# A two-layer hybrid network: modulation weights in 512 KB halves, output weights split over the last attention head, the dt turn one z block later

## The chip, the cores and the metric

The kernel runs on one core of one Trainium2 chip. The metric is the device time of one execution in microseconds. Engines are TensorE (PE; its weight loads are PEld), VectorE (DVE), ScalarE (ACT), GpSimd (POOL) and SyncE (SP, which here only issues transfers). ScalarE issues transfers too, in the order of its other instructions.

## The reference

The network has two layers on 256 context and 1024 latent tokens of width 1024. Before each layer a modulation vector is computed from a conditioning vector, for latent and for context tokens:

```
def modulation(cvec, w, b):
    m = jax.nn.silu(cvec) @ w + b
    return jnp.split(m, 3, axis=-1)          # shift, scale, gate
...
u_lat = rms_norm(h_lat, g_pre[i]) * (1.0 + sc[:, None]) + sh[:, None]
...
h_lat = h_lat + gt[:, None] * rms_norm(y_lat, g_post[i])
```

Layer 0 projects u with one weight matrix into six parts. Two (xr, gr) feed a gated linear recurrence in both directions (four tiles of 128 channels), four (q, k, v, gd) a differential attention with four heads:

```
s = jnp.einsum("bqhcd,bkhcd->bhcqk", q, k).astype(jnp.float32) * (DA_HEAD_DIM ** -0.5)
p = jax.nn.softmax(s, axis=-1)
w = p[:, :, 0] - lam * p[:, :, 1]
...
y_l = jnp.concatenate([r_l * jax.nn.silu(gr_l), head_norm(o_l) * jax.nn.silu(gd_l)], axis=-1) @ w_out
```

Layer 1 projects into z, x, B, C and dt (dt through a softplus) and runs a chunked state-space scan (32 heads, chunks of 128) in both directions, then a gated norm and an output projection. The output is the latent stream.

## The kernel before

Arithmetic is float32. A projection (`proj`, line 321) makes three products per weight tile: operand and weight are each split in a high part, which TensorE multiplies in its faster 32-bit format, and a low remainder: high x high, low x high and high x low. The names end in H and L, or begin with wh and wl. Each output block of 512 tokens is 24 such matmuls of 512 columns, the context block 24 of 256 columns. The split itself is a cast on ScalarE (line 298) and a subtraction on VectorE (line 299), after a 512 KB load on SyncE into a two-buffer staging pool (`wst`).

The order of each engine's instructions is made by a list scheduler with a cost model, from the program's text; pools with a set number of buffers, in SBUF and PSUM, make an instruction wait until the last reader of a buffer's former tile is done. On the chip every engine and every issuing queue works in the order it was given.

`backbone` first computes the modulation of layer 0 (`modulation`, lines 135 to 184), then u, then the four recurrence tiles (`lru_in`, `lru_scan`). Between the first two scans the text has `gate_rows` (lines 187 to 205), which computes the gate part of both layers' modulation, and after the second scan the rest of layer 1's modulation. Both make, per step k of 8, four products of 32 stationary columns each (the conditioning vectors, padded) with 512 weight columns; product j writes partitions 32j to 32j + 31 of one PSUM tile and uses only 32 of TensorE's columns. They are plain float32, so each is two records in the trace. Each of the four weight tiles of a step is a 256 KB load on SyncE into the pool `wmod1` with five buffers. The tail of `gate_rows` handles four pieces of 512 columns: copy from PSUM, add the bias, multiply by the post-norm weight (both loaded by ScalarE's queue into the single buffer `gbm`), store to DRAM on SyncE. The piece's own tile has the tag "u" with one buffer, and so has the row `mrow` that layer 1's modulation copies out of PSUM before TensorE transposes it (line 170).

`v_block` (line 473) projects v and transposes it in three groups, each into a PSUM tile of the rotating `c.psum`; for head 0 it first issues one dummy matmul (`fill`, line 228).

`attention_head` (lines 530 to 641) goes over ten query tiles: scores, row maxima on VectorE (lines 578, 579, 583), exponentials on ScalarE (585, 586), the weighted difference on VectorE (598), transposes (608) and the product with v (612). In the last head, `between()` runs once, at query tile 5: it issues the last gate block (`gd_block`, whose matmuls serve as work between tiles), closes the pools of layer 0's inputs, and loads and splits the eight row blocks of the output weights, 512 KB each through two staging buffers: cast on VectorE (line 1427), remainder on GpSimd (line 1428).

In layer 1, `dt_block` (lines 658 to 725) computes the dt tables and returns `turn`, which transposes them (line 717); the text has one `z_block` ahead of `turn` and seven behind it.

Of the kernel before, what the change touches and what calls it, by code (L numbers as in the profile page):

```python
# [19 lines left out]
P = 128  # L20
# [113 lines left out]

def modulation(c, a, layer, wpool, tmp, ahead=None, between=None):
# [9 lines left out]
    for hf in range(parts):  # L145
        pm = c.pm()
        for k in range(KT):
# [6 lines left out]
            else:  # L154
                for j in range(4):
                    wm = wpool.tile([P, cw], F32, name=f"wm{layer}_{j}{k}", tag="wm")
                    nc.sync.dma_start(wm, src[:, j // 2, cw * (j % 2) : cw * (j % 2) + cw])
                    cols.append(wm)
            if ahead:
                ahead(hf, k)  # L160
            for j in range(4):
                w = cols[j // 2][:, cw * (j % 2) : cw * (j % 2) + cw] if parts == 2 else cols[j]
                nc.tensor.matmul(pm[32 * j : 32 * j + 32, 0:cw], c.sc[:, k, :], w, start=(k == 0), stop=(k == KT - 1))
# [7 lines left out]
        if layer == 0 and hf == 0:  # L171
            c.turned = last_pe(nc)
        pv = pc[:, 0:cw].rearrange("p (q j r) -> p j q r", q=nq, r=32)
# [13 lines left out]
def gate_rows(c, a, wpool, tmp):  # L187
    nc = c.nc
    pm = c.pm()
    for k in range(KT):  # L190
        for j in range(4):
            w = wpool.tile([P, 512], F32, name=f"wg{j}_{k}", tag="wm")
            o = 2 * D + 512 * (j % 2)
            nc.sync.dma_start(w, a["w_mod"][j // 2, k * P : (k + 1) * P, o : o + 512])
            nc.tensor.matmul(pm[32 * j : 32 * j + 32, :], c.sc[:, k, :], w, start=(k == 0), stop=(k == KT - 1))
    for j in range(4):
        layer, n = j // 2, slice(512 * (j % 2), 512 * (j % 2) + 512)
        row = tmp.tile([P, 512], F32, name=f"grow{j}", tag="u", bufs=1)[0:2, :]
        nc.vector.tensor_copy(row, pm[32 * j : 32 * j + 2, :])
        for q, src, op in ((0, a["b_mod"][layer : layer + 1, 2 * D + n.start : 2 * D + n.stop], OP.add),  # L200
                           (1, a["g_post"][layer : layer + 1, n], OP.mult)):
            bm = tmp.tile([2, 512], F32, name=f"gbm{j}{q}", tag="gbm", bufs=1)
            nc.scalar.dma_start(bm, src.to_broadcast([2, 512]))
# [269 lines left out]
def v_block(c, w, uH, uL, pool, apool, name):  # L473
# [4 lines left out]
    for j0, n in ((0, 4), (4, 4), (8, 2)):  # L478
        ps = c.psum()
        if name == "0" and j0 == 0:  # L480
            fill(c, ps, FILL[3])
# [48 lines left out]
def attention_head(c, h, kk, v, pool, spool, scores, dr, between=None):  # L530
# [105 lines left out]
    for qt in range(NT):  # L636
        nxt = front(qt + 1) if qt + 1 < NT else None
        if qt == 5 and between:
            between()
        back(qt, weigh(qt, *fr))  # L640
        fr = nxt
# [160 lines left out]
def layer1(c, a, uH, uL, U, out, dram, h_d, psm, xdt):  # L802
# [17 lines left out]
    with ExitStack() as s1:  # L820
        c.wpools = [(U.enter_context(tc.tile_pool(name=f"wst1{i}", bufs=1)), U.enter_context(tc.tile_pool(name=f"wsp1{i}", bufs=1))) for i in range(2)]
        c.wcyc = 0
        with tc.tile_pool(name="dtp", bufs=1, side="right") as dp:
            tabs, turn = dt_block(c, a, xdt, dp, scst, dr)
            z_block(c, a, 0, uH, uL, zp, dr)
# [3 lines left out]
        for i in range(1, nz):  # L829
# [743 lines left out]
```

## Time and profile before

| quantity | value |
|---|---|
| median of 3 runs | 1819.09 us (1819.03 to 1819.13) |
| profiled execution | 1822.81 us |
| its span | 1820.8 us |
| mean granted TensorE clock | 0.987 of full speed |
| TensorE / VectorE / ScalarE / GpSimd busy | 1749.1 / 1136.4 / 814.3 / 497.1 us |

The span is the stretch from the first to the last recorded instruction; the execution's own time is 2 us longer. Busy time of TensorE counts pipelined matmuls with their modelled ends, so one record may be longer than the distance to the next. A row's bracket names the idle time of the engine just before it and what released it.

### The profile page before, as it was taken

Reading aid. Unit: us, or ns where it says so; the run is one execution under the profiler, and the core shown is the slowest. Engines: PE = TensorE matmul, PEld = TensorE weight load, DVE = VectorE, ACT = ScalarE, POOL = GpSimd, SP = SyncE. Lnnn points to the kernel's source line nnn. Section 1 sums busy time; section 2 is a strip of 40 time slices with the busy share of each in tenths; the row PEclk is TensorE's granted clock in tenths of the full one; section 3 lists DMA queues with packets and bytes.
Section 4 is the critical chain, followed back from the end, with each engine's and each line's share of the span. In section 5 each row is a group of like instructions: output and inputs, shape, how many; then the busy total and the mean of one; then the engine's idle time right before and its main releaser. Section 6 shows DMA issues by size and latency. Waiting matters only on the chain. (4 is left out here: it accounts for less than half of the span.)

```text
span 1820.8 us, 24369 instructions
## 1 busy us (share of the span) xinstructions
PE 1749.1 (96%) x8968; PEld 1344.8 (74%) x8968; DVE 1136.4 (62%) x1646; ACT 814.3 (45%) x1599; POOL 497.1 (27%) x467
## 2 busy tenths in 40 slices
PE   6999999999999997999999999999999899999997
PEld 2665377788888886886788888888787577776765
DVE  3735366785838577566736767666221766778797
ACT  4542455374636464444434444445311554343443
POOL 1201000100000004110006766767401443443342
PEclk8999999999999998999999999999999999999999
DMA  7434513532222315342235757576954677776664
GB/s 246 149 100 150 174 61 123 148 93 76 90 58 70 102 44 179 116 139 81 85 112 157 233 156 231 159 217 168 317 176 139 222 247 248 258 265 244 243 228 140
DMA packets 269244, 293.44 MB, mean 161 GB/s; under 512 B 16905, under 2 KB 213518, under 8 KB 268614
## 3 DMA queue, kind: packets, MB, share of 16 engines
q1 hardware_dynamic: 240944, 262.73, 45.7%
q10 hardware_dynamic: 28182, 29.16, 4.9%
q8 instruction: 71, 1.16, 0.3%
q14 instruction: 47, 0.39, 0.1%
HBM read 187.49 MB, written 100.42 MB: 158 GB/s over the span
## 5 line engine op out<-in xcount | busy, mean ns | idle before, releaser
L350 DVE SCALAR_TENSOR_TENSOR xbc<-xp_xb,pb,xbc 128x1283 f32<-128x1283 f32 (+1 forms) x72 | 141.7, 1972 | 2.8
L769 POOL TENSOR_TENSOR x2w<-tok_x,wd 128x1152 f32<-128x1152 f32 (+2 forms) x48 | 119.2, 2508 | 48.3 <-ACT tok_x L749 48.3
L967 POOL TENSOR_TENSOR s<-s,etb 128x512 f32<-128x512 f32 x64 | 69.2, 1082 | 184.5 <-DVE s L968 91.6
L623 POOL TENSOR_TENSOR ors<-z,mhalf 128x4 f32<-128x4 f32 (+1 forms) x12 | 13.8, 1146 | 351.9 <-DVE z L621 285.3
L1146 PE MATMUL psap<-wo1l,yh 128*128 128x512 f32 x256 | 101.6, 397 | 3.2 <-DVE wo1l L1040 3.2
L778 POOL TENSOR_TENSOR x2l<-x2w,x2h 128x1152 fp32r<-128x1152 f32 x32 | 103.6, 3258 | 0.5 <-DMA d_x<-x2l 0.5
L348 DVE TENSOR_SCALAR xbc<-xp_xb,pb 128x1283 f32<-128x1283 f32 (+1 forms) x24 | 29.9, 1245 | 116.2 <-ACT xp_xb L340 94.3
L1146 PE MATMUL psap<-wo1h,yh 128*128 128x512 f32 x256 | 101.8, 400 | 0.2 <-DVE acc L1156 0.2
L1146 PE MATMUL psap<-wo1h,yl 128*128 128x512 f32 x256 | 101.5, 396 | 0.0
L321 PE MATMUL pscp<-u1H,wh_xb 128*128 128x512 f32 x232 | 92.2, 398 | 0.0
L321 PE MATMUL pscp<-u1H,wl_xb 128*128 128x512 f32 x232 | 92.0, 397 | 0.0
L321 PE MATMUL pscp<-u1L,wh_xb 128*128 128x512 f32 x232 | 91.8, 396 | 0.0
L968 DVE TENSOR_TENSOR s<-s,psat 128x512 f32<-128x512 f32 x64 | 43.6, 681 | 74.0 <-PE psat L956 71.2
L321 PE MATMUL psap<-u1H,wl_z 128*128 128x512 f32 x224 | 89.3, 399 | 0.0
L321 PE MATMUL psap<-u1L,wh_z 128*128 128x512 f32 x224 | 89.2, 398 | 0.0
L321 PE MATMUL psap<-u1H,wh_z 128*128 128x512 f32 x224 | 89.2, 398 | 0.0
L585 ACT ACTIVATE p<-scores,nm 128x1024 f32<-128x1024 f32 x64 | 71.5, 1117 | 29.5 <-DVE nm L584 20.3
L560 PE MATMUL scores<-kk,xq 128*128 128x512 f32 (+1 forms) x208 | 77.4, 384 | 1.7 <-ACT p L585 1.5
L777 ACT CAST x2h<-x2w 128x1152 fp32r<-128x1152 f32 x32 | 37.2, 1161 | 89.2 <-POOL x2w L769 89.2
L956 PE MATMUL psat<-x,bk 128*128 128x512 f32 x216 | 72.1, 437 | 2.5 <-DMA x<-d_x 1.2
L561 PE MATMUL scores<-kk,xl 128*128 128x512 f32 (+1 forms) x208 | 72.9, 364 | 0.0
L612 PE MATMUL psat<-v,wT 128*128 128x128 f32 x572 | 71.4, 278 | 0.0
(487 smaller groups left out, 5115.0 us busy)
## 6 DMA issues: line engine op xcount, KB each, us to landing
x<-d_x SPq DMA_DIRECT2D x72, 512.0 KB
d_x<-x2h SPq DMA_DIRECT2D x32, 576.0 KB
d_x<-x2l SPq DMA_DIRECT2D x32, 576.0 KB
wst_xb<-in_o_w_in_dram SPq DMA_DIRECT2D x24, 512.0 KB
d_acc<-acc SPq DMA_DIRECT2D x24, 512.0 KB
acc<-d_acc SPq DMA_DIRECT2D x24, 512.0 KB
wm<-in_w_mod_dram SPq DMA_DIRECT2D x16, 512.0 KB
wg<-in_w_mod_dram SPq DMA_DIRECT2D x32, 256.0 KB
```

The costliest lines, as they stand in the source:

```text
L321: nc.tensor.matmul(ps[:n, :w_], l[:, k, :], r[:, k, t0 : t0 + w_], start=(k == 0 and i == 0), stop=(k == KT - 1 and i == 2))
L350: nc.vector.scalar_tensor_tensor(out[:, j0 : j0 + n], xp[:, j0 + k : j0 + k + n], cw(k), out[:, j0 : j0 + n], OP.mult, OP.add)
L560: nc.tensor.matmul(out, xq[m][:, qs], kk[m][:, k0 : k0 + n], start=True, stop=False)
L561: nc.tensor.matmul(out, xl[:, m, qs], kk[m][:, k0 : k0 + n], start=False, stop=True)
L585: nc.scalar.activation(pr[m][:, NCTX:], scores[m], AF.Exp, bias=nm[:, m : m + 1], accum_out=zz[:, 1, m : m + 1])
L612: nc.tensor.matmul(po[:, :P], wT[:, j, :], v[:, j, :], start=(j == 0), stop=(j == nkt - 1))
L769: nc.gpsimd.tensor_tensor(x2[:, o : o + n, :].rearrange("p c (h e) -> p c h e", e=64), t[:, a0:a1, :].rearrange("p c (h e) -> p c h e", e=64),
L778: nc.gpsimd.tensor_tensor(l, x2, h.bitcast(F32), OP.subtract)
L956: nc.tensor.matmul(ps, bk[:, l, t, :], x2[:, r, :], start=(i == 0), stop=(i == 2))
L967: nc.gpsimd.tensor_tensor(sn, self.prev[g, d], self.et[:, hs, t : t + 1].to_broadcast([P, 8, 64]), OP.mult)
L968: nc.vector.tensor_tensor(sn, sn, psv, OP.add)
L1146: nc.tensor.matmul(po, l[:, q, :], w[:, n], start=(q == 0 and i == 0), stop=(q == 3 and i == 2))
```

## The change

It has seven parts.

1. Modulation of layer 1 and gate rows load per step two tiles of 512 KB [128 x 1024] instead of four of 256 KB; the pool `wmod1` has three buffers instead of five. A new function `together` issues product 2 first and asks the scheduler to put products 3, 0 and 1 right behind it.
2. The tail of `gate_rows` handles eight pieces of 256 columns instead of four of 512. The bias row and the post-norm row are loaded into the second half of the piece's own tile; `gbm` is gone.
3. One dummy matmul (`FILL[3]` is 1) moves from `v_block` of head 0 to the end of layer 0's modulation.
4. The third group of transposes of `v_block` of head 0 goes to a tile of `c.pm()`.
5. In the last head the gate block and the pools open at query tile 3, and the eight weight blocks are issued at tiles 3 to 8.
6. Their high part is cast by ScalarE, their remainder subtracted by VectorE.
7. Two z blocks stand ahead of the dt `turn` in the text.

```diff
+def together(c, product):
+    product(2)
+    with c.tc.issue_after(last_pe(c.nc)):
+        for j in (3, 0, 1):
+            product(j)
...
-                for j in range(4):
-                    wm = wpool.tile([P, cw], F32, name=f"wm{layer}_{j}{k}", tag="wm")
-                    nc.sync.dma_start(wm, src[:, j // 2, cw * (j % 2) : cw * (j % 2) + cw])
+                for i in range(2):
+                    wm = wpool.tile([P, D], F32, name=f"wm{layer}_{i}{k}", tag="wm")
+                    nc.sync.dma_start(wm, src[:, i, :])
                     cols.append(wm)
...
         if layer == 0 and hf == 0:
             c.turned = last_pe(nc)
+        elif layer == 0:
+            fill(c, c.pm(), FILL[3])
...
-    for j in range(4):
-        layer, n = j // 2, slice(512 * (j % 2), 512 * (j % 2) + 512)
-        row = tmp.tile([P, 512], F32, name=f"grow{j}", tag="u", bufs=1)[0:2, :]
-        nc.vector.tensor_copy(row, pm[32 * j : 32 * j + 2, :])
+    for j, o in ((j, o) for j in range(4) for o in (0, 256)):
+        layer, n = j // 2, slice(512 * (j % 2) + o, 512 * (j % 2) + o + 256)
+        t = tmp.tile([P, 512], F32, name=f"grow{j}{o}", tag="u", bufs=1)
+        row = t[0:2, 0:256]
+        nc.vector.tensor_copy(row, pm[32 * j : 32 * j + 2, o : o + 256])
         for q, src, op in ((0, a["b_mod"][layer : layer + 1, 2 * D + n.start : 2 * D + n.stop], OP.add),
                            (1, a["g_post"][layer : layer + 1, n], OP.mult)):
-            bm = tmp.tile([2, 512], F32, name=f"gbm{j}{q}", tag="gbm", bufs=1)
-            nc.scalar.dma_start(bm, src.to_broadcast([2, 512]))
+            bm = t[0:2, 256:512]
+            nc.scalar.dma_start(bm, src.to_broadcast([2, 256]))
             nc.vector.tensor_tensor(row, row, bm, op)
...
     for j0, n in ((0, 4), (4, 4), (8, 2)):
-        ps = c.psum()
-        if name == "0" and j0 == 0:
-            fill(c, ps, FILL[3])
+        ps = c.pm() if name == "0" and j0 == 8 else c.psum()
...
-        if qt == 5 and between:
-            between()
+        if between:
+            between(qt)
...
-            z_block(c, a, 0, uH, uL, zp, dr)
+            for i in range(2):
+                z_block(c, a, i, uH, uL, zp, dr)
...
-    wm = s4.enter_context(tc.tile_pool(name="wmod1", bufs=5))
+    wm = s4.enter_context(tc.tile_pool(name="wmod1", bufs=3))
...
-        for k in range(KT):
-            st = W.mp.tile([P, D], F32, name=f"wos{k}", tag="xr")
-            nc.sync.dma_start(st, wo[:, k, :])
-            nc.vector.tensor_copy(W.h[:, k, :], st)
-            nc.gpsimd.tensor_tensor(W.l[:, k, :], st, W.h[:, k, :].bitcast(F32), OP.subtract)
+
+    def split_wo(k):
+        st = W.mp.tile([P, D], F32, name=f"wos{k}", tag="xr")
+        nc.sync.dma_start(st, wo[:, k, :])
+        nc.scalar.copy(W.h[:, k, :], st)
+        nc.vector.tensor_tensor(W.l[:, k, :], st, W.h[:, k, :].bitcast(F32), OP.subtract)
+
+    def last_head(qt):
+        if qt == 3:
+            open_out()
+        for k in {3: (0,), 4: (1,), 5: (2,), 6: (3, 4), 7: (5, 6), 8: (7,)}.get(qt, ()):
+            split_wo(k)
```

Three places show how the instructions move. Line numbers of the changed kernel are some 13 to 23 higher. First TensorE in the gate rows, at step k = 3 of before: wg0_3 to wg3_3 are the step's four weight tiles, psbp is the projection of the third recurrence tile.

```order
L195 MATMUL psat57_1111<-wg0_3_1148,silu_c_125 32x512
L195 MATMUL psat57_1111<-wg1_3_1151,silu_c_125 32x512
L321 MATMUL psbp58_1255<-u0L_75,wh_xr2_1251 128x256
L321 MATMUL psbp59_1281<-u0H_74,wh_xr2_1251 128x512
L321 MATMUL psbp59_1281<-u0H_74,wl_xr2_1252 128x512
L321 MATMUL psbp59_1281<-u0L_75,wh_xr2_1251 128x512
L195 MATMUL psat57_1111<-wg2_3_1154,silu_c_125 32x512
L321 MATMUL psbp59_1281<-u0H_74,wh_xr2_1251 128x512
L321 MATMUL psbp59_1281<-u0H_74,wl_xr2_1252 128x512
L321 MATMUL psbp59_1281<-u0L_75,wh_xr2_1251 128x512
L195 MATMUL psat57_1111<-wg3_3_1157,silu_c_125 32x512
```

The same step after, where wg1_3 holds the columns of products 2 and 3 and wg0_3 those of 0 and 1:

```order
L338 MATMUL psbp60_1271<-u0H_74,wh_xr2_1241 128x512
L338 MATMUL psbp60_1271<-u0H_74,wl_xr2_1242 128x512
L338 MATMUL psbp60_1271<-u0L_75,wh_xr2_1241 128x512
L208 MATMUL psbm58_1113<-wg1_3_1140,silu_c_125 32x512 x2
L208 MATMUL psbm58_1113<-wg0_3_1138,silu_c_125 32x512 x2
L338 MATMUL psbp60_1271<-u0H_74,wh_xr2_1241 128x512
L338 MATMUL psbp60_1271<-u0H_74,wl_xr2_1242 128x512
```

The four products, in three runs before, stand in one run. Over both stages the 20 and 22 runs become 9 and 10, and between two runs of the steady part stand 12 to 15 matmuls of the projection.

Second VectorE at the tail of the gate rows. Before, with the pieces grow0 and grow1:

```order
L199 COPY grow0_1208<-psat57_1111 2x512
L442 TENSOR_TENSOR a200_1088<-a200_1088,sg_gr0_488 128x1024
L204 TENSOR_TENSOR grow0_1208<-grow0_1208,gbm00_1210 2x512
L348 TENSOR_SCALAR xc2_1333<-xp_xr2_1244,pa_116 128x1283
L299 TENSOR_TENSOR wl_xr3_1636<-wst_xr3_1633,wh_xr3_1635 128x1024
L350 SCALAR_TENSOR_TENSOR xc2_1333<-xp_xr2_1244,pa_116,xc2_1333 128x1283
L358 SCALAR_TENSOR_TENSOR sg_gr2_1248<-th_gr2_0_1369,psbp61_1344 128x256
L350 SCALAR_TENSOR_TENSOR xc2_1333<-xp_xr2_1244,pa_116,xc2_1333 128x1283
L204 TENSOR_TENSOR grow0_1208<-grow0_1208,gbm01_1213 2x512
```

After, with the pieces grow00 and grow0256, halves of the former first piece:

```order
L216 COPY grow00_1178<-psbm58_1113 2x256
L367 SCALAR_TENSOR_TENSOR xc2_1323<-xp_xr2_1234,pa_116,xc2_1323 128x1283
L221 TENSOR_TENSOR grow00_1178<-grow00_1178 2x256
L367 SCALAR_TENSOR_TENSOR xc2_1323<-xp_xr2_1234,pa_116,xc2_1323 128x1283
L375 SCALAR_TENSOR_TENSOR sg_gr2_1238<-th_gr2_0_1359,psbp62_1334 128x256
L316 TENSOR_TENSOR wl_xr3_1594<-wst_xr3_1591,wh_xr3_1593 128x1024
L221 TENSOR_TENSOR grow00_1178<-grow00_1178 2x256
L375 SCALAR_TENSOR_TENSOR sg_gr2_1238<-th_gr2_256_1387,psbp63_1362 128x512
L216 COPY grow0256_1185<-psbm58_1113 2x256
```

The operand gbm is gone, since the loaded row lies in the piece's own tile; eight such sequences run down VectorE's list, the last of them behind the rotary work of head 0's queries. On TensorE the transposes of the modulation's row, 12 projection matmuls behind the last run before, stand 127 instructions behind it.

Third VectorE in the last head. Before, around query tile 8 (nl and nm are row maxima, wos0 a staged weight block):

```order
L578 TENSOR_REDUCE nl3_8_0_6079<-scores0_2385 128x1
L1427 CAST wo0H_5885<-wos0_5893 128x1024
L594 TENSOR_TENSOR Z3_5442<-zz3_7_5976 128x2
L596 RECIPROCAL rz3_7_6091<-Z3_5442 128x1
L1427 CAST wo0H_5885<-wos1_5897 128x1024
```

After, where the first weight block is met at query tiles 5 and 6:

```order
L599 TENSOR_TENSOR nm3_5_5755<-nm3_5_5755,nl3_5_1_5772 128x1
L1445 TENSOR_TENSOR wo0L_5708<-wos0_5715,wo0H_5707 128x1024
L628 COPY oall3_5397<-psap301_5808 128x128
L593 TENSOR_REDUCE nl3_6_0_5847<-scores0_2342 128x1
L1445 TENSOR_TENSOR wo0L_5708<-wos1_5782,wo0H_5707 128x1024
```

The first two blocks move up by some two query tiles. At the dt turn the order of the transposes among TensorE's instructions is the same in both kernels: they stand behind the matmuls of four z blocks.

## Rows read from the trace of the kernel before

**Rows 1.** Page of before, part 1: engine, busy us (share of the span), instructions.

```profile
PE 1749.1 (96%) x8968; PEld 1344.8 (74%) x8968; DVE 1136.4 (62%) x1646; ACT 814.3 (45%) x1599; POOL 497.1 (27%) x467
```

**Rows 2.** Timeline of PE, gate-row products: start, us, line, operation.

```profile
152.80 0.40 PE L321 MATMUL psbp<-u0H,wl_xr 128*128 128x512 f32 x1
153.03 0.40 PE L321 MATMUL psbp<-u0L,wh_xr 128*128 128x512 f32 x1
153.36 1.05 PE L195 MATMUL psat<-wg,silu_c 128*32 128x512 f32 x4
154.34 0.50 PE L321 MATMUL psbp<-u0H,wh_xr 128*128 128x512 f32 x1
154.68 0.39 PE L321 MATMUL psbp<-u0H,wl_xr 128*128 128x512 f32 x1
```

**Rows 3.** Timeline of PE: a block of four products; two gate products.

```profile
184.16 1.06 PE L163 MATMUL psbm<-wm,silu_c 128*32 128x512 f32 x8
...
119.70 1.99 PE L415 MATMUL psbt<-xc,bdi 128*128 128x512 f32 x4
```

**Rows 4.** Lines 195 and 163: count, ns min/median/max, first and last start.

```profile
L195 PE MATMUL psat<-wg,silu_c x64: 592/592/617, 121.6 to 163.4; 128*32 128x512 f32 x64
...
L163 PE MATMUL psbm<-wm,silu_c x64: 592/605/617, 182.1 to 227.8; 128*32 128x512 f32 x64
```

**Rows 5.** Timeline, two large transfers (640 and 512 KB) and their waiters.

```profile
681.10 0.32 SPq L524 DMA_DIRECT2D d_sgd<-sg_gd  x1
684.09 0.81 SPq L1426 DMA_DIRECT2D wos<-in_e_w_out_dram  x2
...
693.30 3.33 SPq L1426 DMA_DIRECT2D wos<-in_e_w_out_dram  x2
...
700.30 2.78 DVE L1427 CAST wo0H<-wos 128x1024 fp32r<-128x1024 f32 x1 [0.20 <-DMA wos<-in_e_w_out_dram]
```

**Rows 6.** Timeline, 4 KB transfers of the gate-row pieces and their waiters.

```profile
185.10 0.40 ACTq L203 DMA_DIRECT2D gbm<-in_g_post_dram  x1
...
187.63 0.68 DVE L204 TENSOR_TENSOR grow<-grow,gbm 2x512 f32<-2x512 f32 x1 [1.14 <-DMA gbm<-in_g_post_dram]
192.62 0.69 DVE L199 COPY grow<-psat 2x512 f32<-2x512 f32 x1 [4.31 <-DMA d_grow<-grow]
...
190.44 0.26 SPq L205 DMA_DIRECT2D d_grow<-grow  x1
...
203.67 0.45 SPq L205 DMA_DIRECT2D d_grow<-grow  x1
```

**Rows 7.** Timeline of PE, stops around the second scan and the value block.

```profile
279.00 0.50 PE L321 MATMUL psbp<-u0H,wh_gd 128*128 128x512 f32 x1 [3.04 <-DVE sg_gd L358]
...
331.53 0.48 PE L483 MATMUL psbt<-ident,vt 128*128 128x128 f32 x2 [2.65 <-ACT v L484]
```

**Rows 8.** Timeline of PE, first projection of layer 0.

```profile
56.42 0.39 PE L321 MATMUL psbp<-u0H,wh_xr 128*128 128x256 f32 x1 [1.16 <-ACT u0H L259]
```

**Rows 9.** Timeline of DVE, last head: casts, a slowed operation, a subtract.

```profile
690.11 0.68 DVE L1427 CAST wo0H<-wos 128x1024 fp32r<-128x1024 f32 x1
690.98 2.84 DVE L1427 CAST wo0H<-wos 128x1024 fp32r<-128x1024 f32 x1
...
713.74 2.26 DVE L619 SCALAR_TENSOR_TENSOR z<-Z 128x4 f32<-128x4 f32 x1
...
717.76 1.21 DVE L1443 TENSOR_TENSOR mx<-mx,mh 128x1024 fp32r<-128x1024 f32 x1
```

**Rows 10.** Window of the last head: length, PE, PEld, DVE, ACT, POOL, clock, DMA.

```profile
690.00:720.00 30.00, 20.54 (x106) 17.04 (x105) 29.21 (x38) 13.13 (x32) 15.46 (x7) 0.79 0.54 173
```

**Rows 11.** Timeline of ACT, last head: its wait before the last square.

```profile
725.15 0.31 ACT L615 ACTIVATE oj<-oall 128x128 f32<-128x128 f32 x1 [3.96 <-POOL wo0L L1428]
```

**Rows 12.** Timeline of PE, first transposes of the dt tables.

```profile
903.12 0.40 PE L717 MATMUL pscu<-ident,rmask 64*128 64x64 f32 x3 [1.43 <-ACT rmask L702]
```

More of the change, by code (lines that the diff above doesn't have):

```diff
@@ L160, in modulation, with product @@
                 ahead(hf, k)
-            for j in range(4):
-                w = cols[j // 2][:, cw * (j % 2) : cw * (j % 2) + cw] if parts == 2 else cols[j]
-                nc.tensor.matmul(pm[32 * j : 32 * j + 32, 0:cw], c.sc[:, k, :], w, start=(k == 0), stop=(k == KT - 1))
+            def product(j):
+                nc.tensor.matmul(pm[32 * j : 32 * j + 32, 0:cw], c.sc[:, k, :], cols[j // 2][:, cw * (j % 2) : cw * (j % 2) + cw],
+                                 start=(k == 0), stop=(k == KT - 1))
+            together(c, product)
         mrow = tmp.tile([P, 512], F32, name=f"mrow{layer}{hf}", tag="u")[:, 0:cw]
@@ L190, in gate_rows, with product @@
     for k in range(KT):
[L191 to L196, printed above, removed]
-        layer, n = j // 2, slice(512 * (j % 2), 512 * (j % 2) + 512)
-        row = tmp.tile([P, 512], F32, name=f"grow{j}", tag="u", bufs=1)[0:2, :]
-        nc.vector.tensor_copy(row, pm[32 * j : 32 * j + 2, :])
+        wm = []
+        for layer in range(2):
+            w = wpool.tile([P, D], F32, name=f"wg{layer}_{k}", tag="wm")
+            nc.sync.dma_start(w, a["w_mod"][layer, k * P : (k + 1) * P, 2 * D : 3 * D])
+            wm.append(w)
+        def product(j):
+            nc.tensor.matmul(pm[32 * j : 32 * j + 32, :], c.sc[:, k, :], wm[j // 2][:, 512 * (j % 2) : 512 * (j % 2) + 512],
+                             start=(k == 0), stop=(k == KT - 1))
+        together(c, product)
+    for j, o in ((j, o) for j in range(4) for o in (0, 256)):
[3 more added lines that the diff above has]
+        nc.vector.tensor_copy(row, pm[32 * j : 32 * j + 2, o : o + 256])
         for q, src, op in ((0, a["b_mod"][layer : layer + 1, 2 * D + n.start : 2 * D + n.stop], OP.add),
                            (1, a["g_post"][layer : layer + 1, n], OP.mult)):
-            bm = tmp.tile([2, 512], F32, name=f"gbm{j}{q}", tag="gbm", bufs=1)
-            nc.scalar.dma_start(bm, src.to_broadcast([2, 512]))
+            bm = t[0:2, 256:512]
+            nc.scalar.dma_start(bm, src.to_broadcast([2, 256]))
             nc.vector.tensor_tensor(row, row, bm, op)
@@ L828, in layer1 @@
         pool = s1.enter_context(tc.tile_pool(name="p1", bufs=2, side="right"))
-        for i in range(1, nz):
+        for i in range(2, nz):
             z_block(c, a, i, uH, uL, zp, dr)
@@ L1410, in pat3, with open_out @@
         return pAp()
-    def last_head():
+    def open_out():
         gd_block(c, a, HEADS - 1, uH, uL, qp, dr)
```

## The prediction

> **What bounds the kernel now.** I read the page's busy shares first: TensorE works 1749.1 of 1820.8 us, VectorE 62% [rows 1]. So the kernel is bound by TensorE in most stages, and a change can gain only where TensorE's own work shrinks or where TensorE stands still. The list of TensorE's work by line and its timeline give the first kind of place, its waits the second. For each edit I then asked which of the two it touches.
>
> *Small products.* Lines 195 and 163 issue 32 products each, which the trace shows as 64 records each between 121.6 and 227.8 us [rows 4]. In the order of before they stand in 20 and 22 separate runs between the projection's matmuls of line 321. A run costs the same for two products as for four: 1.05 us with 4 records [rows 2], 1.06 with 8 [rows 3]. Its price to the stream: two 512-wide matmuls of line 321 start 0.23 us apart, but with a run between them 154.34 - 153.03 = 1.31, and the next one starts 0.34 later instead of 0.23 [rows 2]. So a run costs 1.08 + 0.11 = 1.19 us.
>
> *Standstills.* In the stages the diff touches, TensorE waits 1.16 us in layer 0 [rows 8], 3.04 and 2.65 us around the third scan and the first value block [rows 7], and in the last head it is busy 20.5 of 30 us while VectorE is busy 29.2 [rows 10]: there VectorE bounds. At the dt turn it waits 1.43 us [rows 12].
>
> **The change part by part.**
>
> *Gate rows and modulation of layer 1.* The order of after has 9 and 10 runs where before had 20 and 22: 11 + 12 = 23 runs fewer, 23 x 1.19 = 27.4 us of TensorE. That is the whole gain to be had, and two things eat from it.
>
> First, the weights now come in 512 KB tiles with three buffers. The second tile of step k+1 goes into the buffer that the first tile of step k leaves at the end of its run, so between the end of one run and the start of the next lies one whole load. The trace bounds such a load: the 640 KB store issued at 681.10 released SyncE at 684.09, 3.0 us; of the loads issued from 693.30 in 3.33 us the second, issued at about 696.2, released its cast at 700.30, 4.1 us [rows 5]. I take 3.5, between them. Between runs the order leaves TensorE 12 to 15 matmuls of 0.23 us (2.8 to 3.5 us), and once, between the second and third run, only seven 256-wide ones of half that (0.8 us). Gate rows: 2.7 us once and five gaps of some 0.7, 6 us; so 13.1 - 6 = 7. Modulation: five gaps of about 0.7, 3.5 us; 14.3 - 3.5 = 11. So with a load of t us the stalls are 10 x (t - 2.8) + (t - 0.8): 4 us at 3.0, 16 at 4.1. The two stages together give 11 to 23, and I take 18.
>
> The Trainium skill, "DMA: Bandwidth & Descriptors", section "Anatomy of one DMA", fits a transfer (there issued by GpSimd) as 2.0 us fixed plus bytes at 436 GB/s. For 512 KB that is an estimate of 3.2 us, inside the bounds above, and by it the two stages would give some 21 instead of 18. The same fixed part speaks against cutting the gate rows finer, since each added piece pays it three times; the 4 KB transfers of this trace, 2.2 and 2.5 us [rows 6], bear it out.
>
> Second, the tail of the gate rows. It was 4 pieces, now 8, and its one buffer now holds the bias row too, so per piece three transfers follow each other: load 2.5, add, load 2.5, multiply, store 2.2 [rows 6]; with two operations of some 0.3 us 7.8 us per piece, 62 us for eight. Both loads are issued by ScalarE, the store by SyncE, each in the queue's turn: a load waits behind ScalarE's gate activations and they behind it, the weight tiles of the modulation stand behind the stores on SyncE. The modulation's row takes the same buffer and waits for the eighth store; TensorE's transposes wait for that row. In the order of after these transposes stand far back: from the last gate-row run to the last modulation run I count 49 us of work plus 3.5 of stalls, and from there 91 512-wide matmuls (21 us), 24 256-wide (3) and 12 gate products (9.6, at 1.92 us for two [rows 3]), 33.5 us; together 86 us. The tail has 86 / 8 = 10.7 us per piece. Before, two stores lay 13.2 us apart (190.44 and 203.67) [rows 6], where SyncE was held by weight loads. Following the queues piece by piece I get the eighth store some 80 us after the last run, so the transposes wait little. But VectorE does the modulation's shift, the third scan's steps and the rotary work in a row behind it, and TensorE's projection buffers wait for the latter: I put a stop of 5.5 us there. It takes the place of the 3.04 at 279.00 [rows 7], so 2.5 net, and 3.5 more for ScalarE and SyncE being held by the serial loads. Tail: -6, bounds 0 and -20.
>
> *Value block.* The third group of transposes gets another PSUM tile, so the stop of 2.65 us <-ACT v [rows 7] goes; the dummy matmul in front goes too. What is late next is the copy of the same values on ScalarE. +2 us, bounds 0 and 4.
>
> *Layer 0.* The dummy matmul now stands in the 1.16 us before 56.42 [rows 8]; it takes no time of other work there unless it outlasts the wait. +1, bounds -1 and 2.
>
> *Last head.* Before, VectorE casts the eight weight rows in three pairs of a free (0.68) and a slow cast (2.84), the slow one beside GpSimd's subtract, and the last pair free: 11.8 us; the same neighbour stretches a 4-element operation to 2.26 [rows 9]. After, ScalarE casts and VectorE subtracts, 8 x 1.21 = 9.7 us [rows 9]. VectorE saves about 4 us, and ScalarE no longer waits for GpSimd before its last square (the idle 3.96 [rows 11]), some 1.4 us of it on the path. Against this: the weights are loaded into memory that the last gate block leaves, so the first load still waits for that block's store (681.10 to 684.09 [rows 5]). After, this block ends earlier, but the first subtract stands before the maxima of tile 6 on VectorE, and everything queued behind it (maxima, hence ScalarE's exponentials, hence TensorE's transposes) waits for block, store (3.0), load (3.5) and cast. I reckon this wait at 3 to 5 us. Sum 0, bounds -5 and +8.
>
> *dt turn.* In the source the second z block now stands ahead of the turn. In the order, all five engines' instructions from the dt projection on are the same as before: the scheduler had already put four z blocks ahead of these transposes. The 1.43 us [rows 12] stay. 0.
>
> Sum: 18 - 6 + 2 + 1 + 0 + 0 = 15 us. The profiled execution took 1822.8 us (span 1820.8), its median 1819.1; the same 15 us off give 1807.8 and 1804.
>
> **The rivals.**
> *A, the loads hide.* If a 512 KB load takes 3.0 us and the tail keeps up, 27.4 - 4 + 2 + 1 = 26 us: 1793. For it: the gaps of 2.8 to 3.5 us; against it: the short gap and the loads of 4.1 us.
> *B, the last head gains too.* If the gate block's store is early enough, VectorE's 4 us, the 1.4 and half of TensorE's 9.5 us of idle time come off, 8 more: 1796. For it VectorE at 29.2 of 30 [rows 10]; against it the in-order subtract.
> *C, the loads set the pace.* At 5.1 us per load the stalls are 10 x 2.3 + 4.3 = 27.3 us, all of the gain. The tail then has that much more room and costs only its 2.5, the value block and layer 0 give 3: 1819. Against it: no load among the rows is that long.
> *D, slower: the tail of the gate rows.* Place: the transposes of the modulation's row. Price: 8 x (p - 10.7) us with p the time of a piece. From p = 12.6 it eats the 15 us; at 13.2, the distance of the two stores before [rows 6], it costs 20, and the time is 1804 + 20 = 1824. For it: that distance, and eight pieces through two in-order queues. Against it: the floor of 7.8.
>
> **How the numbers follow.** Forecast 1804 (own range 1798 to 1811): 0.52. A 0.12, B 0.14, C 0.10, D 0.12. What a measurement here can tell from no change is about 0.2%, 3.6 us. Faster: forecast, A, B and a little of C, 0.80; same: most of C and some of D's lower end, 0.10; slower: D, 0.10. Range 1791 to 1818: it takes in A, B and nearly C, and leaves D and a gain over 28 us out.
>
> **What would show it.** Right: 9 and 10 runs of small products, in the steady part 4 to 5 us apart; waits of TensorE on the weight loads under 1 us and one of 2 to 3; the modulation's transposes reached 85 us after the last gate-row run with little wait; a stop of about 5 us after them; no 2.65 us stop at the value block; the same 1.4 us at the dt turn; VectorE in the last head waiting for its first subtract. Wrong: TensorE waiting over 10 us at the transposes, runs 6 us apart, or a last head that changes by more than 5 us.

## The result, and the profile after

The changed kernel took 1800.6 us (median of 4 runs, 1800.42 to 1803.07); the kernel before took 1819.11 us beside it (4 runs, 1819.03 to 1820.54). The ratio is 0.9900 (95% interval 0.9882 to 0.9917): 18.5 us off, forecast 15. The profiled execution took 1800.72 us (span 1798.9), 0.1 above its median, where that of before lay 3.7 above.

The page of the changed kernel, part 1 (engine, busy us, share of the span, instructions), answers to [rows 1]:

```profile
PE 1718.0 (96%) x8968; PEld 1339.0 (74%) x8968; DVE 1133.1 (63%) x1658; ACT 820.1 (46%) x1607; POOL 481.9 (27%) x459
```

TensorE has the same 8968 records and 31.1 us less busy time. So the change took no product away. How much of the time saved the kernel kept is a matter of what TensorE then waited for.

To place the gain I use one stretch throughout: from the first gate-row product to the first transposes of the dt tables. It holds everything the change touches but layer 0, and the same TensorE records in both kernels but for the two of the dummy matmul, which before has inside it. In before these start at 121.62 [rows 4] and 903.12 [rows 12], a stretch of 781.50 us. In the changed kernel (timeline of PE: start, us, line, operation, idle before and its releaser):

```profile
120.63 1.07 PE L208 MATMUL psbm<-wg,silu_c 128*32 128x512 f32 x8
...
882.71 0.83 PE L732 MATMUL pscu<-ident,rmask 64*128 64x64 f32 x10 [1.08 <-ACT rmask L717]
```

That is 762.08, so 19.4 us less. Outside the stretch the executions differ by themselves: the changed kernel and the eight of this study that share its layer 0 have the first row between 118.92 and 123.40. What a layer-0 edit of 1 us is worth can therefore not be read from one profile.

**The small products.** Busy time by line (count | busy us, mean ns | idle before, releaser), from 115 to 260 us, of before and then of the changed kernel:

```profile
L163 PE MATMUL psbm<-wm,silu_c 128*32 128x512 f32 x64 | 23.6, 605 | 0.0
L195 PE MATMUL psat<-wg,silu_c 128*32 128x512 f32 x64 | 22.1, 604 | 0.0
```

```profile
L169 PE MATMUL psat<-wm,silu_c 128*32 128x512 f32 x64 | 10.6, 605 | 4.7 <-DMA wm<-in_w_mod_dram 4.7
L208 PE MATMUL psbm<-wg,silu_c 128*32 128x512 f32 x64 | 9.6, 605 | 4.2 <-DMA wg<-in_w_mod_dram 4.2
```

There are 64 records each, as in [rows 4], now in 9 and 10 runs. Their busy time is 20.2 us instead of 45.7: 25.5 of the 31.1 us. Before, no run waited; now ten of the nineteen wait for a weight load, 8.9 us together. The timeline of PE in the steady part of the gate rows:

```profile
126.58 1.06 PE L208 MATMUL psbm<-wg,silu_c 128*32 128x512 f32 x6
...
129.48 1.04 PE L208 MATMUL psbm<-wg,silu_c 128*32 128x512 f32 x2
131.49 1.06 PE L208 MATMUL psbm<-wg,silu_c 128*32 128x512 f32 x8
137.11 1.06 PE L208 MATMUL psbm<-wg,silu_c 128*32 128x512 f32 x8 [0.91 <-DMA wg<-in_w_mod_dram]
142.10 1.06 PE L208 MATMUL psbm<-wg,silu_c 128*32 128x512 f32 x8 [0.98 <-DMA wg<-in_w_mod_dram]
...
156.34 1.07 PE L208 MATMUL psbm<-wg,silu_c 128*32 128x512 f32 x8 [0.98 <-DMA wg<-in_w_mod_dram]
```

Steady runs are 4.6 to 5.0 us apart. From one run's end to the next one's start there are 142.10 - 138.17 = 3.9 us. Three runs of the modulation wait more than 1 us (1.06, 1.56 and 1.06).

**The tail of the gate rows.** Timeline of SP, the first and one later of the eight stores (the eighth is the end of the row with two, 231.56 + 10.25 = 241.8):

```profile
164.15 0.31 SPq L222 DMA_DIRECT2D d_grow<-grow  x1
...
231.56 10.25 SPq L222 DMA_DIRECT2D d_grow<-grow  x2
```

So the eighth store is out 84 us after the last gate-row run ended at 157.4. Timelines of ACT and PE behind it:

```profile
244.03 0.56 ACT L174 COPY mrow<-psat 128x512 f32<-128x512 f32 x1
```

```profile
245.04 0.60 PE L179 MATMUL psbm<-ident,mrow 128*128 128x128 f32 x4
...
253.72 0.58 PE L338 MATMUL psbp<-u0H,wh_gd 128*128 128x256 f32 x1 [4.79 <-DVE q_q L478]
```

The transposes (L179) show no wait; TensorE reached them 87.6 us after the last gate-row run. The stop of 4.79 behind them stands in the place of the 3.04 of [rows 7]. A smaller one, which before does not have, stands ahead of them:

```profile
220.27 0.50 PE L338 MATMUL psbp<-u0H,wh_gr 128*128 128x512 f32 x1 [1.11 <-DVE sg_gr L375]
```

The longer stop also costs clock. These are windows (length, busy time of PE, PEld, DVE, ACT and POOL, granted clock, DMA share, GB/s) around the 3.04 in before and around the 4.79 in the changed kernel, then four rows of TensorE behind the 4.79:

```profile
274.00:284.00 10.00, 6.96 (x28) 4.77 (x27) 9.22 (x8) 6.80 (x8) 3.60 (x3) 1.00 0.52 200
```

```profile
252.00:258.00 6.00, 4.28 (x20) 4.28 (x21) 6.00 (x9) 3.54 (x6) 5.65 (x2) 0.50 0.04 8
```

```profile
254.10 0.41 PE L338 MATMUL psbp<-u0H,wl_gd 128*128 128x256 f32 x1
254.31 0.41 PE L338 MATMUL psbp<-u0L,wh_gd 128*128 128x256 f32 x1
...
258.41 0.28 PE L338 MATMUL psbp<-u0H,wl_gd 128*128 128x256 f32 x1
258.53 0.28 PE L338 MATMUL psbp<-u0L,wh_gd 128*128 128x256 f32 x1
```

In before the clock stayed at 1.00. In the changed kernel it is 0.50 from 252 to 258, and the 20 matmuls that start there after the stop stand 0.21 us apart instead of the 0.12 at full clock: some 2 us more.

**The value block.** Windows of the changed kernel, as above:

```profile
310.00:320.00 10.00, 10.00 (x53) 8.56 (x52) 6.07 (x11) 2.40 (x4) 0.00 (x0) 1.00 0.71 208
320.00:330.00 10.00, 10.00 (x52) 8.43 (x52) 6.46 (x10) 3.73 (x6) 0.00 (x0) 1.00 0.84 216
```

The stop of 2.65 [rows 7] is gone; TensorE is busy throughout at full clock.

**The last head.** Timelines of DVE, ACT and PE; compare [rows 9 to 11]:

```profile
657.57 1.23 DVE L1445 TENSOR_TENSOR wo0L<-wos,wo0H 128x1024 fp32r<-128x1024 f32 x1 [2.63 <-DMA xq<-d_qH]
```

```profile
662.73 1.04 ACT L1444 CAST wo0H<-wos 128x1024 fp32r<-128x1024 f32 x1 [3.29 <-DMA wos<-in_e_w_out_dram]
```

```profile
664.93 0.80 PE L575 MATMUL scores<-kk,xq 128*128 128x512 f32 x1 [5.43 <-ACT p L600]
...
684.43 0.50 PE L575 MATMUL scores<-kk,xq 128*128 128x512 f32 x1 [3.20 <-ACT p L600]
```

VectorE waits 2.63 us at its first subtract and ScalarE 3.29 at a cast. (The bracket of the subtract names another transfer, but the subtract starts as ScalarE's cast of the first block ends, at 656.49 + 1.05 = 657.54 us.) The exponentials queued behind the cast come late, and TensorE waits 5.43 and 3.20 for them. The weights' work is cheaper and spread, but it now stands in front of the softmax in two queues.

### The profile page after: what moved, and what is told of

Same layout as the page of the kernel before. It is cut to its first block, busy times and chain, and to the rows that moved or that the text cites. A ratio compares the mean times of both kernels' runs of the same rounds, so it can differ in the third digit from the quotient of the medians.

```text
span 1798.9 us, 24332 instructions
## 1 busy us (share of the span) xinstructions
PE 1718.0 (96%) x8968; PEld 1339.0 (74%) x8968; DVE 1133.1 (63%) x1658; ACT 820.1 (46%) x1607; POOL 481.9 (27%) x459
## 5 line engine op out<-in xcount | busy, mean ns | idle before, releaser
L600 ACT ACTIVATE p<-scores,nm 128x1024 f32<-128x1024 f32 x64 | 71.5, 1117 | 29.0 <-DVE nm L599 17.8
L1087 ACT ACTIVATE td<-xk,cf 128x64 f32<-128x64 f32 x256 | 65.8, 337 | 6.5 <-DVE cf L1084 6.4
```

Of the source, the lines that this page charges most:

```text
L600: nc.scalar.activation(pr[m][:, NCTX:], scores[m], AF.Exp, bias=nm[:, m : m + 1], accum_out=zz[:, 1, m : m + 1])
L1087: nc.scalar.activation(td[:, h, :], xk[:, h, :], AF.Copy, scale=cf[:, h : h + 1])
```

## The experiments

Each kernel ran five rounds beside the kernel before, whose medians there were 1820.6 to 1821.6, where beside the changed kernel it was 1819.1. So medians of different sessions are to be compared through their ratios, which are to before, with 95% intervals; "stretch" is the one above, from one execution each: 781.50 us in before and 762.08 in the changed kernel.

| label | median us | ratio | stretch us |
|---|---|---|---|
| e1_gate_mod_alone | 1803.95 | 0.9916 (0.9902 to 0.9930) | 765.96 |
| e2_rest_alone | 1816.55 | 0.9980 (0.9968 to 0.9991) | 777.31 |
| e3_value_psum_old | 1801.50 | 0.9906 (0.9892 to 0.9920) | 766.29 |
| e4_last_head_old | 1800.77 | 0.9897 (0.9883 to 0.9910) | 761.33 |
| e5_runs_apart | 1801.01 | 0.9884 (0.9867 to 0.9902) | 763.51 |
| e6_sixteen_pieces | 1854.05 | 1.0174 (1.0156 to 1.0192) | 817.83 |
| e7_blocks_later | 1802.41 | 0.9886 (0.9864 to 0.9907) | 763.73 |
| e8_loads_on_gpsimd | 1797.32 | 0.9870 (0.9847 to 0.9893) | 757.04 |
| e9_gpsimd_loads_and_blocks_later | 1800.71 | 0.9885 (0.9868 to 0.9901) | 762.11 |
| e10_four_pieces | 1798.22 | 0.9880 (0.9861 to 0.9899) | 758.96 |
| e11_four_pieces_blocks_later | 1800.88 | 0.9885 (0.9869 to 0.9900) | 762.53 |

How far can one execution be trusted? From the first gate-row product to the first transposes of v, the changed kernel and the three others with its code there took 181.7 to 182.9 us; from the first scores of head 0 to the end of the stretch, six kernels with its last head (sixteen pieces left out) took 556.7 to 558.8. So a difference of 2 us in the whole stretch says little, and where it matters the text below gives the part that the edit touches.

**Gate rows and modulation alone**: parts 1 and 2 of the change; the rest, the last head and the z blocks too, as before. Against the changed kernel:

```diff
-        elif layer == 0:
-            fill(c, c.pm(), FILL[3])
...
-        ps = c.pm() if name == "0" and j0 == 8 else c.psum()
+        ps = c.psum()
+        if name == "0" and j0 == 0:
+            fill(c, ps, FILL[3])
...
-        nc.scalar.copy(W.h[:, k, :], st)
+            nc.vector.tensor_copy(W.h[:, k, :], st)
```

> The kernel before with only the gate rows and layer 1's modulation changed (512 KB halves, three buffers, four products in one run, tail in eight pieces). Theory: 23 runs of small products fewer at 1.19 us are 27.4 us, of which waits on the weight loads take about 9 and the stop behind the tail (4.8 us in place of 3.0, and what the serial loads hold up) about 4 to 5; so 12 to 14 us off, 1805 to 1807, with the stop of 2.65 us at the value block still there. Rival (the stages are linked and the whole gain comes from here): 18 us off, 1801. Rival (the tail eats the gain): under 5 us off, 1815 or more.

It is 16.6 us below the 1820.58 of before in its session, more than the 12 to 14 expected, and the stretch is 15.5 shorter. Up to the first transposes of v, where the two kernels have the same TensorE records, it took 183.6 us instead of 197.9, so 14.3 of the gain lie there. The value block still stops TensorE (2.16 us).

**The rest alone**: the changed kernel with `gate_rows`, the modulation and the pool `wmod1` of before:

```diff
-            for i in range(2):
-                wm = wpool.tile([P, D], F32, name=f"wm{layer}_{i}{k}", tag="wm")
+            for j in range(4):
+                wm = wpool.tile([P, cw], F32, name=f"wm{layer}_{j}{k}", tag="wm")
...
-    wm = s4.enter_context(tc.tile_pool(name="wmod1", bufs=3))
+    wm = s4.enter_context(tc.tile_pool(name="wmod1", bufs=5))
```

> The changed kernel with gate rows and modulation as before. Theory: layer 0 gives 1 us, the value block 5 to 7 (its stop of 2.65, the half clock behind it and the dummy matmul), last head and dt turn nothing: 6 to 8 us off before, 1811 to 1813. Rival (my predicted sizes): 3 us off, 1816. Rival (the last head gains once the stages ahead are left alone): over 10 us off, 1809 or less.

4.0 us below before, not the 6 to 8 expected but near the 3 of the first rival; the stretch is 4.2 shorter. The two halves add up: 15.5 + 4.2 = 19.7 beside the 19.4 of the whole change. So four fifths of the gain is the small products with their tail.

**The value block's third PSUM tile undone**:

```diff
-        ps = c.pm() if name == "0" and j0 == 8 else c.psum()
+        ps = c.psum()
```

> The changed kernel with the third group of transposes of head 0's value block back in its former PSUM tile. Theory: the stop on the copy of the values comes back, 2.65 us, and with it a stretch of half clock that cost about 1.7 us: 3 to 5 us over the changed kernel. Rival (something else is late right behind, so that the stop is only moved): within 1 us of it.

The stop is back (timeline of PE, then a window, of this kernel):

```profile
314.64 0.69 PE L498 MATMUL psbt<-ident,vt 128*128 128x128 f32 x2 [2.07 <-ACT v L499]
```

```profile
310.00:320.00 10.00, 7.93 (x30) 6.21 (x29) 3.25 (x6) 1.45 (x3) 0.00 (x0) 0.83 0.81 216
```

The stretch is 766.29 - 762.08 = 4.2 us longer, as much as the second experiment gained. 3.8 of it lie between the first transposes of v and the first scores of head 0, which hold the same records in both. Timelines of PE, the changed kernel and then this one:

```profile
303.17 1.28 PE L498 MATMUL psbt<-ident,vt 128*128 128x128 f32 x8
...
323.90 0.28 PE L575 MATMUL scores<-kk,xq 128*128 128x256 f32 x1
```

```profile
301.84 1.27 PE L498 MATMUL psbt<-ident,vt 128*128 128x128 f32 x8
...
326.41 0.28 PE L575 MATMUL scores<-kk,xq 128*128 128x256 f32 x1
```

Two more pairs differ in this stop: before and the rest alone (23.88 against 21.25 us), and gate rows and modulation alone against the changed kernel (23.60 against 20.73). With the four 512-wide matmuls that stand in this part only where the stop is gone (0.9 us), they give 3.5 and 3.8. So stops of 2.07 to 2.65 us cost 3.5 to 3.8 here. The clock adds to the stop itself: in this kernel the mean granted clock of the slice is 0.83, which is a third of it (3.4 us) at the lower of TensorE's two levels, 1.2 instead of 2.4 GHz, or 1.7 us of lost work. The median moved by only 0.9. The stretch before the first gate-row product was 1.7 us shorter in this execution and the one behind the dt turn 2.6 shorter than in the changed kernel's, which this edit does not touch; the medians' intervals hold both sizes. So the edit is worth 3.5 to 3.8 us where it stands, which the medians neither show nor exclude.

**The last head of before** (gate block and weight blocks at query tile 5, VectorE casts, GpSimd subtracts):

```diff
-        if between:
-            between(qt)
+        if qt == 5 and between:
+            between()
...
-        nc.scalar.copy(W.h[:, k, :], st)
-        nc.vector.tensor_tensor(W.l[:, k, :], st, W.h[:, k, :].bitcast(F32), OP.subtract)
+            nc.vector.tensor_copy(W.h[:, k, :], st)
+            nc.gpsimd.tensor_tensor(W.l[:, k, :], st, W.h[:, k, :].bitcast(F32), OP.subtract)
```

> The changed kernel with the last head as before (all eight blocks issued at query tile 5, cast on VectorE, remainder on GpSimd). Theory: the new split gains on VectorE what it loses on the wait for its first block, so the time is that of the changed kernel within 1.5 us. Rival (the split is worth the 4 us that VectorE saves and more): 4 to 8 us over it. Rival (its early wait costs): 3 to 5 us under it.

1800.77 against 1800.6, stretch 0.8 shorter: parts 5 and 6 of the change are worth nothing that can be measured, as expected.

**The products of a step not kept together** (so 14 and 13 runs, the larger tiles kept):

```diff
-    product(2)
-    with c.tc.issue_after(last_pe(c.nc)):
-        for j in (3, 0, 1):
-            product(j)
+    for j in range(4):
+        product(j)
```

> The changed kernel with the four products of a step issued in text order 0 to 3 and not held together: the order then has 14 and 13 runs where the changed kernel has 9 and 10. Theory (each run costs the stream 1.19 us): 8 runs more are 9.5 us, less what of the 9 us of waits on weight loads the spread hides, so 3 to 9 us over the changed kernel. Rival (the halves and fewer transfers gave the gain, not the runs): within 1.5 us of it.

By line, from 115 to 260 us, of this kernel (its lines stand two higher):

```profile
L206 PE MATMUL psbm<-wg,silu_c 128*32 128x512 f32 x64 | 15.6, 604 | 0.0
L167 PE MATMUL psat<-wm,silu_c 128*32 128x512 f32 x64 | 14.5, 604 | 0.1
```

Busy time is 30.1 instead of 20.2 us and the waits are gone: 9.9 us more work, 8.9 - 0.1 = 8.8 us less waiting. The stretch is 1.4 longer, the median 0.4. I had expected the additional runs to show in the time; in the whole they do not, and the time is the rival's, because they fill the loads' time. It also confirms the price of a run from the other side: 8 more runs x 1.19 = 9.5 us by [rows 2]. The runs are the gain all the same: 27 are 15 fewer than before, 15 x 1.19 = 17.9 us without waits, beside 27.4 - 8.9 = 18.5 with them. So TensorE either works in that time or waits in it. Up to the first transposes of v this kernel took 185.7 us, some 3 more than the 181.7 to 182.9 of the changed kernel's code; head 0 then took 1.5 less. The order that the changed kernel asks of the scheduler gains at most these 3 us over larger tiles alone, and nothing that the medians show.

**Sixteen pieces in the tail**:

```diff
-    for j, o in ((j, o) for j in range(4) for o in (0, 256)):
+    for j, o in ((j, o) for j in range(4) for o in (0, 128, 256, 384)):
```

> The changed kernel with the tail of the gate rows in sixteen pieces of 128 columns. Theory: the pieces are serial, three transfers each, and TensorE reaches the transposes of the modulation's row 88 us after the last gate run; sixteen pieces at 7.8 us (the floor) to 10.5 us (as measured with eight) take 125 to 168 us, so TensorE waits 37 to 80 us there and the kernel takes that much longer. Rival (the tail is not on the path): within 3 us of the changed kernel.

33 us slower than the 1821.37 of before in its session, 53 over the changed kernel, as expected (37 to 80). Timeline of PE:

```profile
310.02 1.12 PE L179 MATMUL psbm<-ident,mrow 128*128 128x128 f32 x4 [38.41 <-ACT mrow L174]
```

Three more stops of 6.07, 4.10 and 2.30 us, for ScalarE's activations of the scans and a load, stand between 246 and 268 us. This is the rival D of the prediction, made to happen: the stores lie (308.4 - 163.5) / 15 = 9.7 us apart, nearly as long as the 11.1 with pieces of twice the size, so the tail has a price per piece and not per byte, and once it outlasts TensorE's 88 us of other work it is on the path.

**The weight blocks later** (two each at tiles 5 to 8):

```diff
-        for k in {3: (0,), 4: (1,), 5: (2,), 6: (3, 4), 7: (5, 6), 8: (7,)}.get(qt, ()):
+        for k in {5: (0, 1), 6: (2, 3), 7: (4, 5), 8: (6, 7)}.get(qt, ()):
```

> The changed kernel with the first weight blocks issued two query tiles later (two blocks each at tiles 5, 6, 7 and 8; the gate block still opens at tile 3). Theory: VectorE no longer stands before the maxima of tile 6 waiting for the first block (2.6 us) nor ScalarE on the third (3.3 us), so 2 to 5 us under the changed kernel. Rival (all eight subtractions then lie in the last 30 us, where VectorE is full): the same time or up to 3 us more.

No gain, where 2 to 5 us were expected: 1802.41, the stretch 1.7 longer, 1.1 of it behind the first scores of head 0. The rival had the time right. The last head itself looked shorter in this trace (113.4 us from the transposes of p at the third head's last query tile to those of the last head's output, instead of 115.9). That was a landmark that moves: from there to the dt turn it took 178.5 instead of 175.0, since matmuls of the output projection that stood in the head's waits now stand behind it.

**The rows loaded by GpSimd**:

```diff
-            nc.scalar.dma_start(bm, src.to_broadcast([2, 256]))
+            nc.gpsimd.dma_start(bm, src.to_broadcast([2, 256]))
```

> The changed kernel with the bias and post-norm rows of the gate tail loaded through GpSimd's queue instead of ScalarE's. Theory: the tail ends sooner, since a load no longer waits behind ScalarE's activations; VectorE's step that stands behind the last piece comes sooner, and the stop of 4.8 us behind the transposes shrinks to 0 to 3: 2 to 5 us under the changed kernel. Rival (the stop is VectorE's own work in a row, whatever the tail does): within 1 us. Rival (GpSimd's queue is the slower one): over it.

The lowest median of all: 1797.32, 3.3 below the changed kernel's (24 below before beside it, where the changed kernel is 18.5 below), the stretch 5.0 shorter. The two ratios' intervals overlap by a little (0.9882 to 0.9893), so the medians alone do not quite prove it. The stretch says the same: up to the first transposes of v it took 178.6 us, and 179.8 in the combination below that has the same tail, against 181.7 to 182.9. So some 3 us are the edit's; 1.1 of the 5.0 lie behind the first scores of head 0, which it does not touch. The waits of VectorE from 157 to 245 us point to ScalarE (engine, line, waited for: us in total, times, longest). The changed kernel, then this one:

```profile
DVE i L445 <- ACT i L433: 9.0, 3, 3.0
```

```profile
DVE i L445 <- ACT i L433: 1.5, 2, 1.0
```

The tail itself is hardly faster; its last rows, timeline of SP and then of PE:

```profile
229.43 8.52 SPq L222 DMA_DIRECT2D d_grow<-grow  x2
```

```profile
241.11 0.60 PE L179 MATMUL psbm<-ident,mrow 128*128 128x128 f32 x4
...
261.74 0.50 PE L338 MATMUL psbp<-u0H,wh_gd 128*128 128x512 f32 x1 [2.60 <-DVE sg_gd L375]
```

The eighth store leaves at 238.0 instead of 241.8. But ScalarE no longer issues loads that wait for VectorE's adds, VectorE waits less for its activations of the scans (L433), and the 4.79 us stop is gone, with the half clock behind it; a stop of 2.60 stays, near the 3.04 of before and like it without loss of clock (1.00 from 258 to 265).

Two things changed at once, though. The scheduler gave this kernel another order, too: the rotary step q_q, which releases TensorE from the 4.79, stands behind the scan steps in VectorE's list of the changed kernel, and ahead of them here. Timelines of DVE, the changed kernel and then this one:

```profile
250.76 2.33 DVE L454 TENSOR_TENSOR_SCAN a<-r,a,T 128x1024 f32<-128x1024 f32 x1
253.00 0.67 DVE L478 TENSOR_TENSOR q_q<-psbp,ropeC_s 128x512 f32<-128x512 f32 x1
```

```profile
245.62 1.27 DVE L478 TENSOR_TENSOR q_q<-psbp,ropeC_s 128x512 f32<-128x512 f32 x2
...
253.25 2.32 DVE L452 TENSOR_TENSOR_SCAN a<-r,a,T 128x1024 f32<-128x1024 f32 x1
```

And with the runs apart VectorE waits little for ScalarE's activations, but a stop is there: q_q waits 2.86 us for the load of its table ropeC_s. Waits of its VectorE, then its timeline of PE:

```profile
DVE i L443 <- ACT i L431: 2.8, 2, 1.7
```

```profile
245.94 0.63 PE L336 MATMUL psbp<-u0H,wh_q 128*128 128x512 f32 x1 [4.52 <-DVE q_q L476]
```

So the GpSimd loads remove the stop, but how much of that is ScalarE's queue and how much the order is not shown; it would take these loads in the changed kernel's order.

**Combinations**: GpSimd loads with the weight blocks later (both edits above), four pieces (below, on the GpSimd loads), and four pieces with the blocks later.

```diff
-    for j, o in ((j, o) for j in range(4) for o in (0, 256)):
+    for j, o in ((j, o) for j in range(4) for o in (0,)):
...
-        row = t[0:2, 0:256]
+        row = t[0:2, 0:512]
...
-            bm = t[0:2, 256:512]
-            nc.gpsimd.dma_start(bm, src.to_broadcast([2, 256]))
+            bm = t[32 + 32 * q : 34 + 32 * q, 0:512]
+            nc.gpsimd.dma_start(bm, src.to_broadcast([2, 512]))
```

> The changed kernel with two edits together: the bias and post-norm rows of the gate tail issued by GpSimd (alone 1797.3 us, 3.3 below the changed kernel) and the eight weight blocks of the last head at query tiles 5 to 8 (alone 1802.4, in its trace the last head 2.5 us shorter). Theory (two stages far apart, gains add): landmarks at the dt turn 5 + 2.5 us earlier than in the changed kernel, some 875 us, and a median of 1795 (1792 to 1798). Rival (what the later blocks save in the last head is given back in the layer after it): 1797 to 1799.

> The changed kernel with the gate tail in four pieces of 512 columns again, without more memory: bias and post-norm rows are loaded by GpSimd into partitions 32 and 64 of the piece's own tile, so both loads of a piece run beside each other. Theory (the tail costs piece count x serial transfers): a piece takes 7 to 9 us, the fourth store is out 30 to 36 us after the last gate-row run, some 190 to 200 us, about 45 us before TensorE reaches the transposes of the modulation's row, so these wait for nothing of the tail; the stop behind them stays away as with the GpSimd loads alone; median 1795 to 1798, and not over 1800. Rival (the stop is set by VectorE's work behind the transposes, not by the tail): the same transposes at 241 us and 1797 to 1799, no gain over the GpSimd loads alone.

> The four pieces with loads beside each other and the weight blocks at query tiles 5 to 8, together. Theory (gains of stages apart add): 2 to 3 us below the four pieces alone, 1793 to 1796. Rival (the last head's gain does not outlast the next layer): within 1 us of the four pieces alone.

The blocks later made both kernels they were added to slower (stretch 762.11 against 757.04, 762.53 against 758.96; medians +3.4 and +2.7, the latter two not beyond their uncertainty). Behind the first scores of head 0, where the blocks lie, the difference is 3.9 and 1.4 us. The medians lie above what theory and rival of both expectations allowed: the hoped-for sum of the gains fails. With four pieces the tail is done early, timelines of SP and PE:

```profile
161.18 0.31 SPq L222 DMA_DIRECT2D d_grow<-grow  x1
...
189.38 0.27 SPq L222 DMA_DIRECT2D d_grow<-grow  x1
```

```profile
209.23 0.62 PE L179 MATMUL psbm<-ident,mrow 128*128 128x128 f32 x4
```

The fourth store leaves 33.5 us after the last gate-row run instead of 84, and the scheduler put the transposes 36 us earlier than in the changed kernel. It gains nothing over the GpSimd loads: 1798.2 against 1797.3, stretch 758.96 against 757.04. So off ScalarE's queue the length of the tail does not matter any more. The rival of that expectation had the time right, though not the transposes, which it left at 241 us. A piece took (189.38 - 161.18) / 3 = 9.4 us, a little more than I had expected.

## Why the prediction was right, and where its sizes were off

*The runs: +18 forecast, 18.5 measured.* The products' price (23 x 1.19 = 27.4) and the waits on loads (4.2 + 4.7 = 8.9 against 9.5) came out as reckoned; the first is reckoned with the price of [rows 2], and runs apart agrees with it (9.9 us for 8 runs). Within it one step failed: the wait of 2.7 us at the third run. The second step had issued three of its products at 126.58 and only the last at 129.48, so the buffer that it read first was free in time, and the run at 131.49 waited for nothing. The other waits were a little longer than the 0.7 us reckoned (mean 0.84 for the gate rows, 0.95 for the modulation), which nearly made it up: the estimate of 3.5 us per load was some 0.2 us low. That all waits would stay under 1 us did not hold.

By the Trainium skill, "DMA: Bandwidth & Descriptors", section "Anatomy of one DMA", the estimate was 3.2 us per load and a gain of 21. This trace does not agree: 3.9 us lay between two steady runs that needed one load.

*The tail: -6 forecast, -2 to -4 left over* (18.5 less 14.3, the first experiment's gain up to the transposes of v, or less 16.5, the difference of the rest alone and the changed kernel there, 198.99 and 182.54). The schedule came out close: eighth store 84 us after the last run (80 reckoned), transposes at 87.6 (86), stop 4.79 (5.5). The net 2.5 of the stop was 1.8. What failed is the further 3.5 us put on the held queues of ScalarE and SyncE: the trace names other things in their place, the stop of 1.1 ahead of the transposes and some 2 us at half clock behind the 4.79, a term that the prediction did not have. These sum to 4.9, above what is left over; the difference is not explained. That the held queues cause the stop is likely, but not shown apart from the order.

*The value block: +2 forecast, 3.5 to 3.8 measured in its stage.* The step counted the stop at less than its length and left out the clock behind it; the mechanism was right. The upper bound was 4.

*Layer 0: +1 forecast, not settled.* The first gate-row product came 1.0 us earlier, but the same code varies over 4.5 us between executions. It was not tried alone.

*Last head: 0 forecast, 0 measured*, by the mechanism named: a wait for store, load and cast in front of the softmax eats VectorE's saving. The wait sat more on ScalarE (3.29) than on VectorE's first subtract (2.63). *dt turn: 0 forecast, 0 measured*: the idle time is 1.08 beside 1.43 [rows 12]; the order was the same. Part 7 of the change had no run of its own, but the first experiment leaves it out and has the same 1.08.

The parts, 14.3 to 16.5 for small products with their tail and 3.5 to 3.8 for the value block, make 17.8 to 20.3, beside 19.4 in the stretch and 18.5 in the medians. So what the forecast lacks lies in the sizes of the tail and the value block. That the runs' 18 came out is in part luck: a wait that did not occur made up for the others. Of the rivals, B came closest in time (1796) and failed on the last head, which gained nothing; its three terms sum to 10, not 8. A (26 us off) failed on the loads, which did not hide; C on loads of 5.1 us, which did not occur; D on its condition: p was 84 / 8 = 10.5 us, just under its 10.7, and sixteen pieces showed what lies beyond.

## What to carry to other kernels

Small matmuls that take a fixed time each run should be counted by runs and not by products, and joining them pays until the loads of their weights set the pace; from there fewer runs only turn work into waiting. A chain of tiny transfers is worth trying on a queue whose engine has nothing urgent: here that gained some 3 us, though the chain itself was hardly shorter. A short stop of TensorE should be priced with the clock behind it. And a stretch between two fixed instructions around the edit tells gains of a few us that medians of a long kernel blur, if no work can move across its ends; how far executions of the same code differ in it has to be measured too.

## What the runs showed that was not expected

- A stop of TensorE of 2.07 us cost 3.8: the granted clock fell to a mean of 0.83 over the 10 us slice, where the same work without the stop ran at 1.00. Behind the 4.79 it was 0.50 for 6 us, but behind the 3.04 of before 1.00: the length of a stop alone does not tell its price.
- The tail's price is per piece: with pieces of 128, 256 and 512 columns two stores lay 9.7, 11.1 ((241.8 - 164.15) / 7) and 9.4 us apart, although the pieces of 512 loaded both rows beside each other (through GpSimd).
- The loads of 512 KB, two per step on SyncE, repeated every 4.6 to 5.0 us in the steady part of the gate rows, some 210 to 230 GB/s, whether TensorE waited for them or (runs apart) not, where a step took 151.00 - 146.33 = 4.67 us.
